# A hybrid decoder layer: two-operand work of the mixer off GpSimd, and early loads kept in program order

## The chip, the cores and the metric

The kernel runs on one core of a Trainium2 chip. The metric is device microseconds of one execution. A core has TensorE (PE: matmul, with its weight loads as PEld), VectorE (DVE), ScalarE (ACT), GpSimd (POOL) and SyncE (SP, which here only issues DMAs). Each engine works through its own instructions in order and waits on semaphores for the others.

## The reference

One layer of a hybrid decoder on 256 prompt tokens and 8 x 4 sample tokens (288 columns, T), width 2048, all in f32:

```python
def layer(x, pos, ssm0, conv0, kbuf, vbuf, mk, mv, lp):
    mix, ... = mixer(rmsnorm(x, lp['norm_mix']), pos, ssm0, conv0, kbuf, vbuf, lp)
    x = x + mix
    x = x + cross_attn(rmsnorm(x, lp['norm_x']), mk, mv, lp)
    x = x + ffn(rmsnorm(x, lp['norm_ffn']), lp)
```

The mixer projects its input to z, a convolution input (x, B, C), dt, q, k and v. Sixteen sliding-window attention heads (2 key heads, window 128, with sinks) and sixteen Mamba-2 heads (two groups, head size 64, state size 128, chunks of 128) run beside each other:

```python
    cs = jnp.cumsum(dtr * a, axis=2)
    wts = cb[..., None] * decay * dtr[:, :, None]
    y_diag = jnp.einsum('bctsgr,bcsgrp->bctgrp', wts, xr)
    to_end = jnp.exp(cs[:, :, -1:] - cs) * dtr
    chunk_states = jnp.einsum('bclgn,bclgrp->bcgrpn', br, xr * to_end[..., None])
    y_off = jnp.einsum('bclgn,bcgrpn->bclgrp', cr, h_starts) * jnp.exp(cs)[..., None]
```

The result is gated by silu(z), normed by group, joined with the attention output and projected by w_out. The outputs include the new states, the last convolution inputs and the key and value windows of prompt and samples. Memory cross-attention and a SwiGLU block of width 5632 follow.

## The kernel before, in words

**Matmul.** Activations stand transposed, one tile of 128 x 288 per 128 channels. Each weight is loaded as f32 (`wload`, line 147, into one of 3 `raw` buffers by SP), split into a rounded part `hi` by ACT (line 156) and a rest `lo` by DVE (through `tt`, line 79), with 4 buffers each, and three matmuls (lines 166 to 168) make one product. A chunk of 1024 weight columns is 24 such matmuls of 128 x 288. PSUM has 4 buffers for the projections (`mm`) and 4 for everything else (`ps`).

**Order.** The program is written out by hand as a chain of projections. Small work is put off by `later(n, fn)`: it runs `n` ticks on, and a tick is one weight chunk (`gemm_w` ends in `step(part=True)`, which takes at most half of what is due). A planner then orders each engine's instructions by priority and by when their inputs are ready: loads of weights stand 4000 places ahead, splits 70 ahead, so a load that needs nothing may be issued long before the place where it is written. SP and POOL are such queues as well: a DMA waits there behind the one ahead of it.

**Start.** `split_x` (line 277) transposes the input, splits it, and copies it (`xst`, 16 `xb` tiles) to be spilled to DRAM (`xspill`) by POOL; the same copies feed the dt product (line 421). The spill is read back into `xT` (line 1022) when the mixer's buffers are free, for the residual.

**Attention heads.** `swa_prompt` (line 494) rotates a pair of heads: shuffle, two products, a sum, the second product on POOL; `scores` follows a tick later, `values` three ticks behind that, `combine` one. `combine` writes `att`, which takes over the slots of `xst`. `swa_sample` (line 566) handles the samples against the cached keys, which it loads itself.

**Mamba heads.** `conv_state` (line 662) loads and transposes the convolution state; `conv_pair` convolves two channel tiles, with POOL copying the borders; `decay` and `decay2` make the masked decay matrices of four heads (POOL multiplies in `cbm`); `ssd` transposes x times dt (`nat_transpose`, line 712), makes the diagonal part (`diag`), has POOL scale it to the chunk's end (`decayed`), and goes on to `states` and `inter`. `sample_state` (line 848) goes over 16 pieces of state (two groups, two halves, four tiles): `load`, `grow` (POOL multiplies the old state by its decay), `trans` (four transposes and the update matmul of 512 columns, line 891, which DVE adds to the grown state), `read` and `add`. Its block-masked B (`bblk`) is masked on POOL and split by two ACT casts and one DVE operation. `part_done` counts the parts of a group; after five come `gate` and `group_norm`.

Of the kernel before, what the change touches and what calls it, by code (L numbers as in the profile page):

```python
# [46 lines left out]
def tile_hymba_step(ctx: ExitStack, tc: tile.TileContext, I: dict, O: list, stop: int = 99):  # L47
# [67 lines left out]
    def transpose(out, in_):  # L115
        k = in_.shape[0]
        b = in_.base_partition() if callable(in_.base_partition) else in_.base_partition
        nc.tensor.transpose(out, in_, ident[b:b + k, 0:k])  # L118

# [157 lines left out]
    def split_x(cp, pcs):  # L277
# [140 lines left out]
    pdt = psum()  # L418
    for k in range(KC):
        j = k % 4  # L420
        nc.tensor.matmul(pdt[32 * j:32 * j + 32, :T], wdt[:, k], xst[k], start=(k < 4), stop=(k >= KC - 4))
    dtT = ts()
    nc.scalar.copy(dtT, pdt[:, :T])
# [33 lines left out]
    def dt_sums():  # L457
# [17 lines left out]
        act(nat[:, 0, 3], pe[:, 48:64], AF.Exp)  # L475
        later(1, lambda: cs_natural(cs))
# [8 lines left out]

    later(1, dt_natural)
    later(7, dt_sums)


# [4 lines left out]
    def swa_prompt(r, pq):  # L494
# [60 lines left out]
        later(1, scores)  # L555
# [9 lines left out]

    def swa_sample():
        ms = cst[:, C_MS:C_MS + 144]
        kcT, vc = [], []
        for hb in range(2):
            k_ = tl(p_ld, [P, 4, P], F32, "ld")  # L570
            nc.sync.dma_start(k_, ck[4 * hb:4 * hb + 4].rearrange("b t g d -> t b (g d)"))
# [78 lines left out]

    later(7, swa_sample)
# [22 lines left out]
    def conv_pair(c0, pcs):  # L674
        ccs = []
        for j in range(2):
# [4 lines left out]
            nc.gpsimd.tensor_copy(smp(xr)[:, :, 0:3], scT[:, c].rearrange("p (b k) -> p b k", k=3))  # L681
# [11 lines left out]
            nc.gpsimd.tensor_copy(cc[:, 0:3], xr[:, 256:259])  # L693
            nc.gpsimd.tensor_copy(cc[:, 3:27].rearrange("p (b k) -> p b k", k=3), smp(xr)[:, :, 4:7])
# [17 lines left out]
    def nat_transpose(c0, h0=None):  # L712
        pts = [psum(), psum()]
        dst = [ts(256), ts(256), ts(256, TS)]
# [5 lines left out]
        for c, ps in enumerate((pts[0][:, 0:256], pts[0][:, 256:512], pts[1][:TS, 0:256])):  # L720
            if h0 is None:
                (nc.scalar.copy if c % 2 else nc.vector.tensor_copy)(dst[c], ps)
            else:
                n = CH[c][1] - CH[c][0]
                tt(nc.vector, hv_(dst[c]), hv_(ps), nat[:n, c, 0, h0:h0 + 4].unsqueeze(2).to_broadcast([n, 4, 64]),
                   ALU.mult)
        return dst

    bnat, cbm = [], []
    cmask = tm().rearrange("p (g b t) -> p g b t", g=2, b=NB)  # L730

    def bc_products():
        bnat.extend(nat_transpose(8))
        for c in range(3):
# [10 lines left out]
        for g in range(2):  # L745
            v = cmask[:, g].rearrange("p b (c t) -> p (b c) t", t=4)[:, 0:64:9]
            nc.gpsimd.tensor_copy(v, xc[10 + g][:, TP:T].rearrange("p (b t) -> p b t", t=4))
# [26 lines left out]
    def decay2(jj):  # L774
        sgv = sgs[jj]
        for c in range(3):
            n = CH[c][1] - CH[c][0]
            tt(nc.gpsimd, sgv[c], sgv[c], cbm[c][:, jj // 2].unsqueeze(1).to_broadcast([n, 4, n]), ALU.mult)

    def ssd(jj):  # L780
        g = jj // 2
        sgv = sgs[jj]
        xnat = nat_transpose(2 * jj, 4 * jj)

        def decayed(src, c, col, n=P):
            o_ = ts(256, n)
            tt(nc.gpsimd, hv_(o_), hv_(src),
               nat[:n, c, col, 4 * jj:4 * jj + 4].unsqueeze(2).to_broadcast([n, 4, 64]), ALU.mult)
            return o_

        def diag():
# [10 lines left out]
            xe = decayed(xnat[0], 0, 2)  # L802
            xe0, xe1 = decayed(xnat[0], 0, 3), decayed(xnat[1], 1, 2)
            xes = decayed(xnat[2], 2, 2, TS)
# [5 lines left out]
            later(2, lambda: states(xe, xe0, xe1))  # L810

        def states(xe, xe0, xe1):
# [634 lines left out]
```

## Time and profile before

| what | us |
|---|---|
| median of 3 timed runs (1396.06 to 1397.71) | 1396.43 |
| the profiled execution | 1390.5 |
| its span, first to last instruction | 1388.7 |
| PE busy in the span | 1367.5 |
| DVE busy | 806.5 |
| ACT busy | 638.0 |
| POOL busy | 177.6 |

The busy time of an engine is the time in which it works on an instruction; matmuls overlap, so PE's is no measure of its peak. In rows of grouped instructions, `out<-in` names the tiles, `xN` the count, then the busy time in us, the mean of one in ns, and the idle time just before with what ended it. Line 79 is the helper `tt`, line 82 `stt`, line 85 `act`, line 118 `transpose`, line 171 `split`.

### The profile page before, as it was taken

Reading aid. Unit: us, or ns where it says so; the run is one execution under the profiler, and the core shown is the slowest. Engines: PE = TensorE matmul, PEld = TensorE weight load, DVE = VectorE, ACT = ScalarE, POOL = GpSimd, SP = SyncE. Lnnn points to the kernel's source line nnn. Section 1 sums busy time; section 2 is a strip of 40 time slices with the busy share of each in tenths; the row PEclk is TensorE's granted clock in tenths of the full one; section 3 lists DMA queues with packets and bytes.
Section 4 is the critical chain, followed back from the end, with each engine's and each line's share of the span. In section 5 each row is a group of like instructions: output and inputs, shape, how many; then the busy total and the mean of one; then the engine's idle time right before and its main releaser. Section 6 shows DMA issues by size and latency. Waiting matters only on the chain.

```text
span 1388.7 us, 26190 instructions
## 1 busy us (share of the span) xinstructions
PE 1367.5 (98%) x10637; PEld 1331.8 (96%) x10637; DVE 806.5 (58%) x1341; ACT 638.0 (46%) x1001; POOL 177.6 (13%) x273
## 2 busy tenths in 40 slices
PE   9999999999999999999999999999999999999997
PEld 8899888988999899999999999999999999999997
DVE  6876798866566459554544544444454544545554
ACT  7455777655455446443343433333343343434332
POOL 4311465413120104000000000000000000000110
PEclk9999999999999999999999999999999999999999
DMA  9655558478557655555555555555555555555552
GB/s 296 169 158 154 143 151 242 134 223 214 165 177 245 221 163 162 167 167 167 168 168 167 168 160 166 167 167 175 167 167 168 167 167 167 168 160 167 167 167 92
DMA packets 249856, 241.17 MB, mean 174 GB/s; under 512 B 12778, under 2 KB 240528, under 8 KB 249736
## 3 DMA queue, kind: packets, MB, share of 16 engines
q1 hardware_dynamic: 246120, 232.43, 54.7%
q0 software_dynamic: 3584, 7.06, 1.7%
q8 instruction: 83, 1.36, 0.4%
q14 instruction: 37, 0.30, 0.1%
q10 hardware_dynamic: 32, 0.01, 0.0%
HBM read 227.59 MB, written 11.85 MB: 172 GB/s over the span
## 4 chain that ended last, share of the span: by engine, by line
PE 78%; DVE 3%; ACT 2%; issue 1%; POOL 1%; DMA 0%; DVEq 0%; ACTq 0%; POOLq 0%
PE mm L167 25%; PE mm L168 25%; PE mm L166 25%; PE ps L118 2%; POOL s L79 1%; DVE lo L79 1%; DVE xa L82 1%; ACT hi L156 0%; PE ps L1151 0%; DMA xT<-xspill 0%; DVE s L82 0%; ACT s L85 0%; POOL m L79 0%; DVE s L79 0%; ACT L85 0%
## 5 line engine op out<-in xcount | busy, mean ns | idle before, releaser
L79 DVE TENSOR_TENSOR lo<-raw,hi 128x1024 fp32r<-128x1024 f32 (+1 forms) x413 | 485.8, 1179 | 462.8 <-ACT hi L156 458.1
L156 ACT CAST hi<-raw 128x1024 fp32r<-128x1024 f32 (+1 forms) x413 | 410.5, 997 | 543.4 <-PE mm L168 442.4
L167 PE MATMUL mm<-xa,hi 128*128 128x288 f32 x2016 | 595.8, 296 | 0.0
L166 PE MATMUL mm<-xa,lo 128*128 128x288 f32 x2016 | 595.0, 295 | 0.6 <-ACT xa L171 0.6
L168 PE MATMUL mm<-xa,hi 128*128 128x288 f32 x2016 | 594.4, 295 | 0.0
L166 PEld LDWEIGHTS mm<-xa,lo 128*128 128x128 f32 x2016 | 380.1, 189 | 5.5 <-issue 3.8
L167 PEld LDWEIGHTS mm<-xa,hi 128*128 128x128 f32 x2016 | 378.8, 188 | 1.1 <-issue 0.7
L168 PEld LDWEIGHTS mm<-xa,hi 128*128 128x128 f32 x2016 | 378.7, 188 | 0.5 <-issue 0.3
L79 POOL TENSOR_TENSOR ssum<-ssum,ls 128x288 f32<-128x288 f32 x43 | 47.3, 1100 | 878.3 <-ACT ls L85 877.5
L166 PE MATMUL mm<-ls,lo 128*128 128x288 f32 x512 | 151.7, 296 | 0.0
L168 PE MATMUL mm<-ls,hi 128*128 128x288 f32 x512 | 151.4, 296 | 0.0
L167 PE MATMUL mm<-ls,hi 128*128 128x288 f32 x512 | 151.3, 295 | 0.0
L166 PE MATMUL mm<-xb,lo 128*128 128x288 f32 x448 | 132.8, 297 | 2.6 <-DVE xT L79 2.6
L167 PE MATMUL mm<-xb,hi 128*128 128x288 f32 x448 | 133.4, 298 | 0.0
L168 PE MATMUL mm<-xb,hi 128*128 128x288 f32 x448 | 132.7, 296 | 0.0
L166 PEld LDWEIGHTS mm<-ls,lo 128*128 128x128 f32 x512 | 96.2, 188 | 0.1
L167 PEld LDWEIGHTS mm<-ls,hi 128*128 128x128 f32 x512 | 96.2, 188 | 0.1
L168 PEld LDWEIGHTS mm<-ls,hi 128*128 128x128 f32 x512 | 96.2, 188 | 0.0
L166 PEld LDWEIGHTS mm<-xb,lo 128*128 128x128 f32 x448 | 85.1, 190 | 3.0 <-DVE xT L79 2.8
L168 PEld LDWEIGHTS mm<-xb,hi 128*128 128x128 f32 x448 | 85.3, 190 | 0.2 <-DVE xb L79 0.2
L167 PEld LDWEIGHTS mm<-xb,hi 128*128 128x128 f32 x448 | 84.7, 189 | 0.1
L79 DVE TENSOR_TENSOR xT<-xT,mm 128x288 f32<-128x288 f32 x64 | 28.3, 448 | 42.1 <-PE mm L168 37.5
(304 smaller groups left out, 1200.6 us busy)
## 6 DMA issues: line engine op xcount, KB each, us to landing
raw<-in_w_gate_dram SPq DMA_DIRECT2D x88, 512.0 KB, 3.6
raw<-in_w_up_dram SPq DMA_DIRECT2D x88, 512.0 KB, 3.6
raw<-in_w_down_dram SPq DMA_DIRECT2D x80, 512.0 KB, 3.6
raw<-in_w_in_dram SPq DMA_DIRECT2D x43, 512.0 KB, 3.9
raw<-in_w_in_dram SPq DMA_DIRECT2D x34, 256.0 KB, 4.6
raw<-in_w_out_dram SPq DMA_DIRECT2D x32, 256.0 KB, 4.2
raw<-in_w_out_dram SPq DMA_DIRECT2D x16, 512.0 KB, 3.5
ld<-in_state_ssm_dram SPq DMA_DIRECT2D x16, 256.0 KB, 4.8
```

Source lines behind the costliest of these rows:

```text
L79: eng.tensor_tensor(out=out, in0=in0, in1=in1, op=op)
L82: nc.vector.scalar_tensor_tensor(out=out, in0=in0, scalar=s, in1=in1, op0=op0, op1=op1)
L118: nc.tensor.transpose(out, in_, ident[b:b + k, 0:k])
L156: nc.scalar.copy(h_, src)
L166: nc.tensor.matmul(ps, wl, xh, start=start, stop=False)
L167: nc.tensor.matmul(ps, wh, xh, start=False, stop=False)
L168: nc.tensor.matmul(ps, wh, xl, start=False, stop=stop)
```

## The change

Three things are done. Products and sums of two tensors in the mixer go from POOL to DVE, or are folded into another operation; small copies go from POOL to ACT. The scaled inputs of `ssd` are made directly from the transposes in PSUM (with dt folded into the factors beforehand). The new state of the samples is made by four scalar-tensor-tensor operations of DVE instead of POOL's product and DVE's sum; B is split once for both groups (`b3`) and masked afterwards. And loads are tied to the program's order: `in_turn` puts a DMA behind the instruction written before it on its queue. With that the spill goes from POOL's queue to SP's, and it, the dt product, the cached keys and the first scores get other ticks.

```diff
+    def in_turn(ins):
+        tc.keep_in_program_order(ins)
...
             nc.vector.tensor_copy(st, pss[k][:, :T])
-            nc.gpsimd.dma_start(xspill[cp * 4 + k], st)
             xst.append(st)
...
-    nc.sync.dma_start(wdt[:, :, 0:16], wq[:, :, O_DT:O_DT + 16])
+    in_turn(nc.sync.dma_start(wdt[:, :, 0:16], wq[:, :, O_DT:O_DT + 16]))
...
+    def dt_product():
+        pdt = psum()
+        for k in range(KC):
+            j = k % 4
+            nc.tensor.matmul(pdt[32 * j:32 * j + 32, :T], wdt[:, k], xst[k], start=(k < 4), stop=(k >= KC - 4))
+        nc.scalar.copy(dtT, pdt[:, :T])
+        for k in range(KC):
+            later(1 + k // 2, lambda k=k: in_turn(nc.sync.dma_start(xspill[k], xst[k])))
+        later(1, dt_natural)
+        later(7, dt_sums)
...
+        tt(nc.vector, nat[:, :, 2], nat[:, :, 2], nat[:, :, 0], ALU.mult)
+        tt(nc.vector, nat[:, 0, 3], nat[:, 0, 3], nat[:, 0, 0], ALU.mult)
...
-    later(1, dt_natural)
-    later(7, dt_sums)
+    later(2, dt_product)
...
-        tt(nc.gpsimd, qb, qb, sq, ALU.mult)
+        tt(nc.vector, qb, qb, sq, ALU.mult)
         tt(nc.vector, qa, qa, qb, ALU.add)
-        nc.gpsimd.tensor_copy(qs[:, :, r], qa[:, TP:T].rearrange("p (b t) -> p b t", t=4))
+        nc.scalar.copy(qs[:, :, r], qa[:, TP:T].rearrange("p (b t) -> p b t", t=4))
...
-        later(1, scores)
+        later(2, scores)
...
+    def cache_keys():
+        for hb in range(2):
+            k_ = tl(p_ld, [P, 4, P], F32, "ld")
+            in_turn(nc.sync.dma_start(k_, ck[4 * hb:4 * hb + 4].rearrange("b t g d -> t b (g d)")))
+            kcs.append(k_)
...
+    later(3, cache_keys)
     later(7, swa_sample)
...
-            nc.sync.dma_start(scv[:24], I["state_conv"][0, :, :, 512 * cp:512 * cp + 512].rearrange("b k c -> (b k) c"))
+            in_turn(nc.sync.dma_start(scv[:24], I["state_conv"][0, :, :, 512 * cp:512 * cp + 512].rearrange(
+                "b k c -> (b k) c")))
...
-            nc.gpsimd.tensor_copy(cc[:, 0:3], xr[:, 256:259])
-            nc.gpsimd.tensor_copy(cc[:, 3:27].rearrange("p (b k) -> p b k", k=3), smp(xr)[:, :, 4:7])
+            nc.scalar.copy(cc[:, 0:3], xr[:, 256:259])
+            nc.scalar.copy(cc[:, 3:27].rearrange("p (b k) -> p b k", k=3), smp(xr)[:, :, 4:7])
...
+        for c, col in ((0, 0), (1, 0), (2, 0)) if h0 is None else NATS:
...
+                tt(nc.vector, hv_(d), hv_(ps), nat[:n, c, col, h0:h0 + 4].unsqueeze(2).to_broadcast([n, 4, 64]),
                    ALU.mult)
...
+    NATS = ((0, 0), (1, 0), (2, 0), (0, 2), (0, 3), (1, 2), (2, 2))
...
+        nc.scalar.copy(b3[0:32], bnat[2])
+        nc.scalar.copy(b3[32:64], bnat[2])
+        tt(nc.vector, b3[64:96], bnat[2], f32(b3[0:32]), ALU.subtract)
...
-            tt(nc.gpsimd, sgv[c], sgv[c], cbm[c][:, jj // 2].unsqueeze(1).to_broadcast([n, 4, n]), ALU.mult)
+            tt(nc.vector, sgv[c], sgv[c], cbm[c][:, jj // 2].unsqueeze(1).to_broadcast([n, 4, n]), ALU.mult)
...
-        xnat = nat_transpose(2 * jj, 4 * jj)
+        *xnat, xe, xe0, xe1, xes = nat_transpose(2 * jj, 4 * jj)
...
-                tt(nc.gpsimd, xc[i][:, P:TP], xc[i][:, P:TP], yo[:, j * P:(j + 1) * P], ALU.add)
+                tt(nc.vector, xc[i][:, P:TP], xc[i][:, P:TP], yo[:, j * P:(j + 1) * P], ALU.add)
...
-                nc.sync.dma_start(h0, ssm[4 * g + i4, :, 4 * hb:4 * hb + 4])
+                ld = nc.sync.dma_start(h0, ssm[4 * g + i4, :, 4 * hb:4 * hb + 4])
+                if g == 0 and hb == 0:
+                    in_turn(ld)
...
+            tt(nc.vector, bblk.rearrange("p (b n) -> p b n", b=4),
+               f32(b3[:, g * P:(g + 1) * P]).unsqueeze(1).to_broadcast([96, 4, P]),
+               bm[:, 4 * hb:4 * hb + 4].unsqueeze(2).to_broadcast([96, 4, P]), ALU.mult)
+            later(2, lambda: trans(hb, h0s, bblk))
...
-                hn = hns[i4]
-                tt(nc.vector, hn, hn, ps, ALU.add)
+                hn = tm()
+                for b in range(4):
+                    e_ = P + 16 * hb + 4 * b + 3
+                    stt(hn[:, b * P:(b + 1) * P], h0[:, b], ecs[i][:, e_:e_ + 1], ps[:, b * P:(b + 1) * P], ALU.mult,
+                        ALU.add)
...
-                tt(nc.gpsimd, xc[i][:, TP:T], xc[i][:, TP:T], yo[:, i4 * TS:i4 * TS + TS], ALU.add)
+                tt(nc.vector, xc[i][:, TP:T], xc[i][:, TP:T], yo[:, i4 * TS:i4 * TS + TS], ALU.add)
```

`swa_sample` then takes its keys from `kcs`; the copies of C into `cmask` and of the convolution state into `xr` go to ACT as well, and `bm` becomes a tile of 96 rows.

More of the change, by code (lines that the diff above doesn't have):

```diff
@@ L719, in nat_transpose @@
                 transpose(o_, xc[c0 + j][:, a:b_])
-        for c, ps in enumerate((pts[0][:, 0:256], pts[0][:, 256:512], pts[1][:TS, 0:256])):
+        dst = []
+        for c, col in ((0, 0), (1, 0), (2, 0)) if h0 is None else NATS:
+            ps = (pts[0][:, 0:256], pts[0][:, 256:512], pts[1][:TS, 0:256])[c]
+            n = CH[c][1] - CH[c][0]
+            d = ts(256, n)
+            dst.append(d)
             if h0 is None:
-                (nc.scalar.copy if c % 2 else nc.vector.tensor_copy)(dst[c], ps)
+                (nc.scalar.copy if c % 2 else nc.vector.tensor_copy)(d, ps)
             else:
-                n = CH[c][1] - CH[c][0]
-                tt(nc.vector, hv_(dst[c]), hv_(ps), nat[:n, c, 0, h0:h0 + 4].unsqueeze(2).to_broadcast([n, 4, 64]),
+                tt(nc.vector, hv_(d), hv_(ps), nat[:n, c, col, h0:h0 + 4].unsqueeze(2).to_broadcast([n, 4, 64]),
                    ALU.mult)
         return dst
+    NATS = ((0, 0), (1, 0), (2, 0), (0, 2), (0, 3), (1, 2), (2, 2))
+    bm = const.tile([96, 8], F32, name="bm")
+    for j in range(3):
+        nc.scalar.copy(bm[32 * j:32 * j + 32], cst[:TS, C_BM:C_BM + 8])
+    b3 = ts(256, 96, F32R)
     bnat, cbm = [], []
@@ L746, in bc_products @@
             v = cmask[:, g].rearrange("p b (c t) -> p (b c) t", t=4)[:, 0:64:9]
[L747 removed]
+            nc.scalar.copy(v, xc[10 + g][:, TP:T].rearrange("p (b t) -> p b t", t=4))
     ecs, xs3 = [None] * 8, [None] * 4
@@ L809, in diag, with states @@
             xs3[jj] = x3_
-            later(2, lambda: states(xe, xe0, xe1))
-        def states(xe, xe0, xe1):
+            later(2, states)
+        def states():
             ps = psum()
@@ L854, in load, with trans @@
                 h0 = tl(p_ld, [P, 4, P], F32, "ld")
[L855 removed]
+                ld = nc.sync.dma_start(h0, ssm[4 * g + i4, :, 4 * hb:4 * hb + 4])
+                if g == 0 and hb == 0:
+                    in_turn(ld)
                 h0s.append(h0)
[L857 to L860 removed]
             bblk = tm(n=96, dt=F32R)
[L862 to L877 removed]
+            tt(nc.vector, bblk.rearrange("p (b n) -> p b n", b=4),
+               f32(b3[:, g * P:(g + 1) * P]).unsqueeze(1).to_broadcast([96, 4, P]),
+               bm[:, 4 * hb:4 * hb + 4].unsqueeze(2).to_broadcast([96, 4, P]), ALU.mult)
+            later(2, lambda: trans(hb, h0s, bblk))
+        def trans(hb, h0s, bblk):
             if hb == 0:
```

39 lines of the change are left out of this document (3 added, 36 removed).

## The prediction, made before the result was known

> **What bounds the kernel now.** The profile's page comes first: the span and the share of each engine.
>
> ```profile
> span 1388.7 us, 26190 instructions
> ...
> PE 1367.5 (98%) x10637; PEld 1331.8 (96%) x10637; DVE 806.5 (58%) x1341; ACT 638.0 (46%) x1001; POOL 177.6 (13%) x273
> ```
>
> TensorE is busy for 98% of the span and no matmul is added or taken away, so the change can win only idle TensorE time: 1388.7 - 1367.5 = 21.2 us at most, plus what idling does to the clock. Next, the busy time by stretch: attention heads (40 to 142), Mamba heads with the output projection's start (142 to 332), and a plain stretch behind them.
>
> ```profile
> 40.00:142.00 102.00, 99.81 (x804) 91.67 (x803) 77.59 (x258) 51.54 (x141) 17.88 (x36) 0.98 0.57 157
> 142.00:332.00 190.00, 179.92 (x1492) 166.19 (x1491) 148.55 (x287) 126.20 (x216) 85.77 (x132) 1.00 0.63 179
> ...
> 360.00:380.00 20.00, 20.00 (x154) 20.00 (x153) 11.23 (x12) 8.39 (x12) 4.59 (x4) 1.00 0.62 172
> ```
>
> The columns are the window, its length, then busy us of PE, weight loads, DVE, ACT, POOL. TensorE idles 2.2 us in the first stretch and 10.1 us in the second. A matmul in the plain stretch takes 20/154 = 0.13 us, so a weight chunk (24 matmuls, one tick) 3.1 us. Third, the waits of TensorE name what it idles for (total, times, longest):
>
> ```profile
> PE mm L166 <- DVE xT L79: 2.6, 1, 2.6
> PE ps L511 <- DVE s L79: 2.2, 1, 2.2
> PE ps L891 <- ACT m L888: 1.7, 1, 1.7
> PE ps L118 <- DVE m L79: 1.4, 2, 0.9
> PE ps L833 <- ACT s L816: 1.3, 2, 0.8
> PE ps L216 <- DVE ld L214: 1.1, 1, 1.1
> PE ps L799 <- DVE s L79: 1.0, 1, 1.0
> PE mm L166 <- ACT xa L171: 0.6, 1, 0.6
> PE ps L943 <- DVE s L79: 0.6, 2, 0.4
> ```
>
> No row with a wait on a split weight (`lo`, `hi`) stands among them. Last, the stretches behind the two longest waits; the ninth number is the granted clock.
>
> ```profile
> 58.80:62.20 3.40, 3.40 (x15) 2.47 (x15) 3.26 (x19) 2.52 (x14) 3.14 (x6) 0.52 0.15 46
> ...
> 331.80:335.20 3.40, 3.40 (x16) 3.40 (x15) 3.40 (x8) 2.15 (x4) 3.38 (x7) 0.51 1.00 282
> ```
>
> Behind each wait over 2 us stand 3.4 us at half clock, which cost 3.4 x 0.48 = 1.6 us more; the 1.7 us wait has none behind it (the clock of 142 to 332 is 1.00, up to the dip at its end). So the wait of the first scores (L511) is worth 2.2 + 1.6 = 3.8 us. The Trainium skill, "TensorE: Matmul & The Clock Gate", section "What's actually happening", has the clock halve after an idle window of about 3.4 us. Here 2.2 us of idleness was enough, so the trace decides.
>
> **The change part by part. The first scores.** Now `scores` follows its projection after two ticks instead of one, its product with `sq` runs on DVE instead of POOL, and the dt product with its 17 small DVE operations begins two ticks later. The wait was for the sum `qa` on DVE. One tick puts 24 matmuls, 3.1 us, in front of the scores, more than the 2.2 us waited; DVE takes 0.451 us for the product (its 128x288 row below), and the hop to POOL and back goes. What comes late next is the dt chain, whose sums are planned seven ticks behind. I take -3.8 us, bounds 0 and -3.8.
>
> **Spill and loads.** The 16 spill writes leave POOL's queue in the first 40 us and go to SP, a tick or more after the dt product, two a tick; cache keys, conv state, dt weights and the first state tiles may no longer be issued ahead of the SP work written before them.
>
> ```profile
> ld<-in_state_ssm_dram SPq DMA_DIRECT2D x16, 256.0 KB, 4.8
> xspill<-xb POOLq DMA_DIRECT2D x16, 144.0 KB, 5.0
> ...
> 1.65 0.89 SPq L274 DMA_DIRECT2D ld<-in_x_prompt_dram  x2
> ...
> SPq L147 <- DVE lo L79: 672.5, 249, 13.1
> ```
>
> SP needs 0.89/2 = 0.45 us per issue, so 16 spills are 7 us of its time in 8 ticks (25 us), and it sits waiting for `raw` buffers (the last row: 672.5 us over the run). A pinned load that waits for an `ld` buffer holds the weight loads behind it; ACT's casts and DVE's splits then wait for those. The cover is three `raw` buffers, 3 x 3.1 = 9.3 us, against 4.8 us to landing. The attention output takes over a spilled tile's slot: head 0 is combined at tick 6, its spill is due at tick 3, 9.4 us against 5.0. I cost all of it at 0; without that cover it costs up to one landing, 4.8 us. The early transfers hold up no matmul now, so their going gains nothing directly.
>
> **POOL's products go to DVE.** Rows of DVE with their forms (count, busy us, mean ns), the second `lo` row from the plain stretch 600 to 750:
>
> ```profile
> L79 DVE TENSOR_TENSOR lo<-raw,hi 128x1024 fp32r<-128x1024 f32 x51 | 69.7, 1371 | 19.9 <-ACT hi L156 19.8
> L79 DVE TENSOR_TENSOR lo<-raw,hi 128x1024 fp32r<-128x1024 f32 x48 | 58.8, 1226 | 71.5 <-ACT hi L156 71.5
> L79 DVE TENSOR_TENSOR lo<-raw,hi 128x512 fp32r<-128x512 f32 x22 | 15.2, 705 | 4.2 <-ACT hi L156 4.2
> L79 DVE TENSOR_TENSOR m<-m,ps 128x512 f32<-128x512 f32 x16 | 10.7, 681 | 4.1 <-PE ps L891 3.9 <-POOL cc L693 0.2
> L79 DVE TENSOR_TENSOR m<-m,m 32x512 fp32r<-32x512 f32 x4 | 4.6, 1146 | 0.1
> L79 DVE TENSOR_TENSOR s<-mm,rstdb 128x288 f32<-128x288 f32 x10 | 4.3, 451 | 0.1
> L82 DVE SCALAR_TENSOR_TENSOR s<-s,hvec,ps 128x288 f32<-128x288 f32 x8 | 3.9, 506 | 0.5 <-PE ps L799 0.5
> L79 DVE TENSOR_TENSOR s<-ps,s 128x256 f32<-128x256 f32 x8 | 3.0, 418 | 2.4 <-PE ps L118 2.4
> L79 DVE TENSOR_TENSOR s<-ps,s 128x128 f32<-128x128 f32 x8 | 2.0, 280 | 6.6 <-PE ps L833 6.6
> L79 DVE TENSOR_TENSOR s<-ps,s 128x32 f32<-128x32 f32 x8 | 1.0, 184 | 1.6 <-PE ps L118 1.6
> ```
>
> Added to DVE between 142 and 332: the masked decay, 8 x 0.705 + 4 of 32x128 at about 0.27 (between the 128x32 and 128x256 rows) = 6.7; the four decayed inputs of each group, straight from PSUM, 16 x 0.418 = 6.7; the inter-chunk and sample sums, 8 x 0.280 + 8 x 0.184 = 3.7; the new state, where one sum of 512 columns becomes four scalar-tensor-tensor operations of 128. That form is not in the trace; 0.506 - (0.451 - 0.280) = 0.335, between 0.280 and 0.506, so 64 x 0.335 - 16 x 0.681 = +10.5. The block-masked B matrix, 4 x (0.705 - 1.146) + 0.4 = -1.4. Together +26.2 us. Back comes what POOL's neighbourhood costs DVE: `lo` takes 1.371 us here and 1.226 where POOL is quiet, 51 x 0.145 = 7.4 us, and more on other forms. DVE goes from 148.6 to about 167 of 190 us, 88%: fuller, not full. In the first stretch 8 x 0.451 = 3.6 us join 77.6 of 102. On ACT some 46 small copies (0.2 us, near its 128x32 row of 217 ns) come and eight casts go:
>
> ```profile
> L85 ACT ACT_TABLE_LOAD x23 | 29.5, 1283 | 0.4
> ...
> L85 ACT ACTIVATE s<-s 128x32 f32<-128x32 f32 x12 | 2.6, 217 | 0.0
> L862 ACT CAST m<-m 32x512 fp32r<-32x512 f32 x4 | 2.5, 612 | 2.0 <-POOL m L79 2.0
> ```
>
> 46 x 0.2 - 8 x 0.61 = +4 us on 126 of 190: hidden.
>
> What TensorE gains is latency. Its waits in the state stages (L891, L118, L833, L799, L943) sum to 1.7 + 1.4 + 1.3 + 1.0 + 0.6 = 6.0 us, and in each the last engine is DVE or ACT, often behind an operation that POOL stretched or fed. Bounds 0 and -6.0; I take half, **-3.0**, since the ACT side (23 table loads, ordered among the copies) stays. Against it stands the sample states' stage: each of the 16 pieces now holds its PSUM buffer for 4 x 0.335 = 1.34 us instead of 0.68. Today's loss there is L891 and L118, 3.1 us; if it grew with the piece it would double. With the stretching gone I take half of that, **+1.6** (bounds 0 and +10.5, all of the added DVE time on TensorE's path).
>
> **The end of the Mamba stage** (0.6 us on L171, 2.6 on `xT`, 1.6 of half clock) hangs on a chain of DVE and ACT operations of the second group norm, then on the loads of the spilled input:
>
> ```profile
> 330.31 0.46 DVE L79 TENSOR_TENSOR xT<-xT,mm 128x288 f32<-128x288 f32 x1 [4.48 <-DMA xT<-xspill]
> ```
>
> The change leaves the chain's tick as it is: 0.
>
> **Sum.** -3.8 - 3.0 + 1.6 = -5.2 us. The profiled execution took 1390.5 us (span 1388.7 and 1.8 around it); it would become 1385.3. The timed runs have a median of 1396.43, 5.9 above the profiled one, so I subtract there: **1391.2 us**.
>
> **Rivals.** *The state stage becomes DVE's (slower).* The price is the added 10.5 us on TensorE's path and two more stretches at half clock, 3.2, against -6.8: +6.9, 1403.3. It decides where fewer than five weight matmuls (0.66/0.13) stand between two pieces in TensorE's order. For it: 0.68 us more for each piece and 88% of DVE; against: a whole DVE stage free of POOL. *The waits only move*: the first scores or the dt chain wait a tick later, the state stages lose as before; 1396. For it: DVE has 81% in the first stretch. *A pinned load lands late* (the change does not bring its order about cheaply): one landing, 4.8, and a half-clock stretch, 1.6, on top of the forecast: 1397.6; against it the 9.3 us of cover. *More goes*: all 6.0 us of waits, and the end's chain comes early enough to lose its 0.6 and its half clock (1.6), without the 1.6 added: 1396.4 - 3.8 - 6.0 - 2.2 = 1384.4. *The clock does not follow the wait*: if the half clock behind the L511 wait has another cause, only 2.2 of the 3.8 go: 1392.8. Two waits over 2 us with two dips right behind them speak against it. The Trainium skill, "TensorE: Matmul & The Clock Gate", section "What's actually happening", would read it so, a wait of 2.2 us being shorter than its window.
>
> **Chances.** Forecast 0.44 (own range 1388.5 to 1394), more goes 0.16, clock does not follow 0.04, waits move 0.14, late load 0.07, slower 0.15. A measurement can tell about 0.2%, 2.8 us, from no change. Faster by that (under 1393.6): 0.42 of the forecast's 0.44 + 0.16 + 0.04 = 0.62; slower (over 1399.2): 0.15 + 0.01 of the late loads = 0.16; the rest, 0.02 + 0.14 + 0.06 = 0.22, is the same. The range reaches to 1384 below and, leaving out the dear half of the slower case, to 1400 above.
>
> **What would show it.** Right: no wait on L511 and no half clock near 60; `lo` near 1226 ns everywhere; L799 and L833 waits under half; the `xT` wait still there. Wrong: L891 or L118 waiting on DVE for over 3 us together, a new wait on a DMA at the conv-state transposes, or TensorE waiting for `lo`. A transfer or a full DVE ahead of the weights would make the prediction wrong altogether.

## The result, and the profile after

The changed kernel took 1381.67 us (median of 4 runs, 1380.41 to 1382.05) against 1396.55 us (4 runs, 1396.06 to 1397.71): a ratio of 0.9897, 95% interval 0.9882 to 0.9911. It gained 14.9 us where 5.2 were forecast, and lies under the range (1384 to 1400). Its profiled execution took 1382.05 us.

The page of the changed kernel, first lines:

```profile
span 1380.3 us, 26140 instructions
...
PE 1367.6 (99%) x10637; PEld 1334.1 (97%) x10637; DVE 810.5 (59%) x1444; ACT 638.4 (46%) x1042; POOL 84.4 (6%) x139
```

TensorE is busy as long as before (1367.5). Its idle time fell from 21.2 to 1380.3 - 1367.6 = 12.7 us. All its waits that are left (total, times, longest):

```profile
PE mm L169 <- DVE xT L79: 2.8, 1, 2.8
PE ps L219 <- DVE ld L217: 1.1, 1, 1.1
PE mm L169 <- ACT xa L174: 0.6, 1, 0.6
PE mm L118 <- DVE ld L1384: 0.2, 1, 0.2
PE ps L954 <- DVE s L79: 0.2, 1, 0.2
```

The first scores' wait and every wait over 0.2 us of the state stages are gone; those of the stage's end, 0.6 and 2.8 us, stayed. (Lines have moved by 3 and more: the weight matmuls of L166 to L168 are now L169 to L171.) By stretch, with the columns as before (PE, weight loads, DVE, ACT, POOL, then the granted clock), and the stretches at and behind the `xT` wait:

```profile
316.00:319.00 3.00, 0.18 (x3) 0.03 (x1) 0.54 (x2) 0.00 (x1) 1.53 (x4) 1.00 1.02 271
319.10:322.50 3.40, 3.33 (x24) 3.10 (x25) 3.40 (x7) 3.00 (x6) 3.40 (x8) 1.00 0.92 245
40.00:142.00 102.00, 102.00 (x842) 95.12 (x842) 82.98 (x274) 58.24 (x162) 11.62 (x25) 1.00 0.63 176
142.00:332.00 190.00, 186.28 (x1550) 173.51 (x1549) 155.47 (x387) 125.72 (x240) 13.03 (x31) 1.00 0.68 196
```

POOL went from 85.77 to 13.03 us in the Mamba stretch; DVE took its products over and rose only from 148.55 to 155.47, where 167 were forecast. TensorE's idle time there is 3.72 us, nearly all of it the `xT` wait and the 0.6 us ahead of it. And behind 2.8 us of waiting the granted clock stayed at 1.00. The groups of DVE that the forecast spoke of:

```profile
L79 DVE TENSOR_TENSOR lo<-raw,hi 128x1024 fp32r<-128x1024 f32 x55 | 66.8, 1217 | 14.3 <-ACT hi L159 14.0
L82 DVE SCALAR_TENSOR_TENSOR m<-ld,s,ps 128x128 f32<-128x128 f32 x64 | 17.5, 342 | 4.6 <-PE ps L899 4.2
```

`lo` has come down from 1371 to 1217 ns, and the new scalar-tensor-tensor form takes 342 ns, where 335 were estimated.

Between the two profiled executions the change gained 1390.5 - 1382.05 = 8.45 us, as much as the idle time fell (8.5). The other 6.4 us lie between the executions that were timed and the one that was profiled, so that was tried first.

### The profile page after: what moved, and what is told of

The parts are those of the page before. It is cut to its first block, busy times and chain, and to the rows that moved or that the text cites. A ratio compares the mean times of both kernels' runs of the same rounds, so it can differ in the third digit from the quotient of the medians.

```text
span 1380.3 us, 26140 instructions
## 1 busy us (share of the span) xinstructions
PE 1367.6 (99%) x10637; PEld 1334.1 (97%) x10637; DVE 810.5 (59%) x1444; ACT 638.4 (46%) x1042; POOL 84.4 (6%) x139
## 4 chain that ended last, share of the span: by engine, by line
PE 96%; DVE 2%; ACT 1%; issue 1%; DMA 0%; POOL 0%; DVEq 0%; ACTq 0%; POOLq 0%
PE mm L169 29%; PE mm L170 29%; PE mm L171 29%; PE ps L118 3%; DVE xa L82 1%; PE ps L823 0%; DVE lo L79 0%; PE ps L521 0%; DMA xT<-xspill 0%; PE ps L1162 0%; ACT hi L159 0%; PE ps L899 0%; PE ps L1197 0%; PE ps L912 0%; PE ps L1235 0%
## 5 line engine op out<-in xcount | busy, mean ns | idle before, releaser
L79 DVE TENSOR_TENSOR lo<-raw,hi 128x1024 fp32r<-128x1024 f32 (+1 forms) x413 | 478.1, 1160 | 449.4 <-ACT hi L159 444.4
L169 PE MATMUL mm<-xa,lo 128*128 128x288 f32 x2016 | 599.8, 298 | 0.6 <-ACT xa L174 0.6
L171 PE MATMUL mm<-xa,hi 128*128 128x288 f32 x2016 | 590.3, 293 | 0.0
L169 PEld LDWEIGHTS mm<-xa,lo 128*128 128x128 f32 x2016 | 378.0, 187 | 4.8 <-issue 3.1
L171 PEld LDWEIGHTS mm<-xa,hi 128*128 128x128 f32 x2016 | 379.1, 188 | 1.0 <-issue 0.7
L169 PE MATMUL mm<-ls,lo 128*128 128x288 f32 x512 | 152.4, 298 | 0.0
L171 PE MATMUL mm<-ls,hi 128*128 128x288 f32 x512 | 151.6, 296 | 0.0
L169 PE MATMUL mm<-xb,lo 128*128 128x288 f32 x448 | 132.2, 295 | 2.9 <-DVE xT L79 2.8
L171 PE MATMUL mm<-xb,hi 128*128 128x288 f32 x448 | 131.9, 294 | 0.0
L169 PEld LDWEIGHTS mm<-ls,lo 128*128 128x128 f32 x512 | 96.6, 189 | 0.1
L171 PEld LDWEIGHTS mm<-ls,hi 128*128 128x128 f32 x512 | 96.3, 188 | 0.0
L169 PEld LDWEIGHTS mm<-xb,lo 128*128 128x128 f32 x448 | 84.6, 189 | 3.6 <-DVE xT L79 3.4
L171 PEld LDWEIGHTS mm<-xb,hi 128*128 128x128 f32 x448 | 84.6, 189 | 0.2 <-DVE xb L79 0.2
```

Of the source, the lines that this page charges most:

```text
L79: eng.tensor_tensor(out=out, in0=in0, in1=in1, op=op)
L169: nc.tensor.matmul(ps, wl, xh, start=start, stop=False)
L171: nc.tensor.matmul(ps, wh, xl, start=False, stop=stop)
```

## The experiments

Each was timed beside the kernel before on the same chip, and each ratio is to that kernel. Its medians there were 1392.79 us (experiments 1 to 4), 1396.54 (5 to 8), 1394.5 (9 to 11) and 1395.57 (12 and 13).

**1. The kernel before, once more.** No edit.

> The kernel before, unchanged. Its timed runs took 1396.5 us, its profiled execution 1390.5; the changed kernel's agree within 2 us. Theory one: the timed executions have more stretches at half clock than the profiled one (a wait of TensorE near 2 us does or does not meet the clock's window); then executions near 1396 show a granted clock under 0.995, by about 12 us of half clock (0.991). Theory two: the waits themselves are longer in them (POOL and DVE meet differently); then the clock stays at 0.995 and the span grows by idle time. Either way the median should be 1396 again.

It took 1391.39 to 1399.21 us (10 runs, median 1396.35). Runs of 1397 us and more had a mean granted clock of 0.992 or 0.993, runs under 1394 one of 0.996 or 0.997. The same kernel beside it, on the same chip, had a median of 1392.79 us (31 runs): two groups of one kernel can lie 3.6 us apart, as they have more or fewer executions at the low clock, so smaller differences between medians below say little by themselves. Its profiled execution took 1398.13 us, 7.6 more than the one shown ahead of the prediction. The waits were the same (`xT` 2.9, first scores 2.8, then 1.7, 1.4, 1.0, 1.0); what differed were stretches at half clock (a granted clock near 0.50). By windows, with the stretch ahead of the second one:

```profile
61.00:64.40 3.40, 3.40 (x15) 2.75 (x15) 3.40 (x23) 3.27 (x16) 2.32 (x4) 0.50 0.18 51
166.80:170.20 3.40, 3.40 (x35) 2.57 (x33) 3.40 (x12) 2.90 (x5) 2.97 (x3) 1.00 0.01 3
170.20:177.00 6.80, 6.80 (x33) 6.04 (x32) 6.80 (x9) 4.84 (x7) 5.33 (x5) 0.50 0.40 105
214.60:218.00 3.40, 3.40 (x15) 3.21 (x14) 3.40 (x2) 2.16 (x4) 3.40 (x5) 0.50 1.01 298
337.40:340.80 3.40, 3.40 (x17) 3.40 (x16) 3.40 (x7) 1.99 (x4) 3.38 (x7) 0.51 0.94 248
...
600.00:800.00 200.00, 200.00 (x1514) 200.00 (x1514) 100.05 (x124) 77.25 (x94) 0.00 (x0) 1.00 0.55 166
```

The four rows at 0.50 and 0.51 add up to 17.0 us at half clock, against 6.8 in the earlier profile: 10.2 x 0.5 = 5.1 us more. The two in the middle, at 170 and 214, stand in the Mamba stretch, where the earlier execution had none. The one at 214 follows the wait of 1.7 us, which had no half clock behind it in the earlier profile; the one at 170 follows no wait, for TensorE counts as busy through all of the 3.4 us ahead of it (30 of its 35 matmuls there are small ones of the sample attention). Most of the rest is in the last row, a stretch of plain weight matmuls, beside the same window of the earlier profile:

```profile
600.00:800.00 200.00, 200.00 (x1528) 200.00 (x1527) 102.56 (x128) 78.82 (x96) 0.00 (x0) 1.00 0.55 169
1000.00:1200.00 200.00, 200.00 (x1527) 200.00 (x1526) 101.49 (x127) 78.92 (x96) 0.00 (x0) 1.00 0.54 167
```

At a clock of 1.00 a matmul takes 200/1528 = 0.1309 or 200/1514 = 0.1321 us there, one of two paces; 14 matmuls fewer are 14 x 0.131 = 1.8 us. So 5.1 + 1.8 = 6.9 of the 7.6 us are found. The kernel before has no single time: it spreads over some 8 us with the stretches at half clock that an execution meets. On all four chips its runs of 1396 us and more had a clock of 0.992 to 0.994, so the first comparison (1396.06 to 1397.71), whose clocks are not known, is taken to have had many too.

**2. The state stages alone**, with the start put back (rotation on POOL, scores after one tick, spill from POOL, dt product at once).

```diff
+            nc.gpsimd.dma_start(xspill[cp * 4 + k], st)
...
-    later(2, dt_product)
+    dt_product()
...
-        tt(nc.vector, qb, qb, sq, ALU.mult)
+        tt(nc.gpsimd, qb, qb, sq, ALU.mult)
...
-        later(2, scores)
+        later(1, scores)
```

> The changed kernel with the attention start put back: spill on POOL in the start, dt product at once, first scores after one tick, rotary product and q copy on POOL. My theory, by waits: the wait of the first scores (2.2 us) and its half clock (1.6) come back and nothing else, 1381.7 + 3.8 = 1385.5. Rival: the start holds most of what the timed runs gained, 1390 or more. Rival: the start is worth nothing by itself, 1382.

1389.65 us (1383.74 to 1394.38), ratio to the kernel before 0.9971 [0.9951, 0.9992]. Waits of TensorE:

```profile
PE mm L169 <- DVE xT L79: 2.8, 1, 2.8
PE ps L611 <- DVE stx L615: 1.4, 1, 1.4
PE ps L520 <- DVE xb L79: 1.2, 1, 1.2
```

No wait over 0.2 us of the Mamba heads' states is left. A wait of 1.4 us is new at the sample attention's scores (L611), with half clock right behind it (149 to 160 us) and again at 173 to 180. At the first scores, near 58 us, only 0.2 us came back, and no half clock (the 1.2 us of L520 stand at 112). So the forecast that their wait alone returns was wrong. The lowest time, 1383.74, came at a clock of 0.997, the highest at 0.991.

**3. The start alone**, in the kernel before.

```diff
-            nc.gpsimd.dma_start(xspill[cp * 4 + k], st)
...
+    later(2, dt_product)
...
-        tt(nc.gpsimd, qb, qb, sq, ALU.mult)
+        tt(nc.vector, qb, qb, sq, ALU.mult)
...
-        later(1, scores)
+        later(2, scores)
```

> The kernel before with only the attention start changed: spill on SP behind the dt product, dt product two ticks on, first scores after two ticks, rotary product on DVE, cached keys pinned. My theory: 3.8 us less than before, 1392.7, with the waits of the state stages as before. Rival (start holds most): 1386 or less. If both parts only work together: 1396.

1394.64 us (1389.78 to 1396.14), ratio 1.0004 [0.999, 1.0017]: nothing gained. Its waits, the largest first:

```profile
PE mm L169 <- DVE xT L79: 2.8, 1, 2.8
PE ps L849 <- ACT s L832: 1.9, 2, 1.1
PE ps L118 <- ACT s L85: 1.8, 2, 1.6
PE ps L907 <- ACT m L904: 1.5, 1, 1.5
...
PE ps L610 <- DVE stx L614: 0.9, 1, 0.9
```

The first scores' wait is gone and there is no half clock near 60. But there is a new wait of 0.9 us at the sample attention (L610), with half clock behind it at 147 to 151 us and again at 168 to 171, and the state stages wait as before. In this profile the loss has moved; why it moves there was not tried.

**4. The changed kernel without any pin** (`in_turn` does nothing).

```diff
-        tc.keep_in_program_order(ins)
+        return ins
```

> The changed kernel with the pins removed: the loads and the spills may again be issued whenever their inputs are there. My theory: the pins are worth nothing on TensorE's path, since weights were never late: 1382 within 2.8 us. Rival: floated loads crowd the first 60 us and delay weights there, and the first wait over 2 us comes back: 1385.5 or more.

1383.84 us (1380.59 to 1392.25), ratio 0.9943 [0.9921, 0.9964]. Three of ten runs took 1389.9 to 1392.25 us, at a clock of 0.991; the profile is of one of these. The other seven took 1380.59 to 1386.89. A wait of 1.1 us stands at L612, and this window behind it (6.8 us more at half clock follow at 171):

```profile
147.00:157.20 10.20, 10.04 (x53) 8.78 (x53) 5.54 (x23) 9.17 (x23) 0.17 (x2) 0.50 0.65 213
```

These are three stretches of 3.4 us in a row, and TensorE counts as busy for 10.04 of the 10.20 us: the second and third follow one in which it hardly idled. Its work there is small matmuls, those of the sample attention above all, among weight matmuls (23 of the 53).

**5. POOL's old products, once more and for nobody.** The changed kernel computes, besides, the masked decay, the scaled inputs and the grown states on POOL into tiles that are not read.

```diff
+            junk = tm()
+            jv = junk[:n, 0:4 * n].rearrange("p (h t) -> p h t", h=4)
+            tt(nc.gpsimd, jv, sgv[c], cbm[c][:, jj // 2].unsqueeze(1).to_broadcast([n, 4, n]), ALU.mult)
...
+            for i4 in range(4):
+                junk = tm()
+                tt(nc.gpsimd, junk.rearrange("p (b n) -> p b n", b=4), h0s[i4],
+                   ecs[4 * g + i4][:, e_:e_ + 13:4].unsqueeze(2).to_broadcast([P, 4, P]), ALU.mult)
```

> The changed kernel with POOL's old products of the Mamba stage (masked decay, scaled inputs, grown states) computed once more on POOL into tiles that nobody reads; everything else as in the changed kernel. Theory one (what POOL does beside DVE stretches DVE and so makes the waits): lo of 128x1024 goes from 1217 ns back to 1330 or more, waits of 0.5 us and over come back in the state stages, 2 to 4 us together, and the time rises by 2 to 5 us at equal clock. Theory two (the waits came from the operations that stood in a chain through POOL): lo is stretched as well, but nothing in the chain is, no wait over 0.4 us comes back in the state stages, and the time changes by less than 1 us.

1397.8 us (1390.79 to 1401.93, 12 runs), ratio 1.0016 [0.9996, 1.0036]: 15.6 us over the changed kernel's 1382.18 on the same chip, three times the most that was expected. The whole gain is lost by work that nothing waits for. Its largest waits:

```profile
PE ps L118 <- DVE s L82: 4.4, 1, 4.4
PE mm L169 <- DVE xT L79: 2.6, 1, 2.6
PE ps L911 <- DVE s L79: 1.3, 1, 1.3
```

`lo` is hardly stretched (1253 ns, not the 1330 expected). Single operations are. The timeline of DVE (start, length in us) shows an addition of two SBUF tiles of 128x128, one that takes 0.28 us elsewhere:

```profile
198.78 6.34 DVE L79 TENSOR_TENSOR s<-s,s 128x128 f32<-128x128 f32 x1
```

and the timeline of POOL the six products that run meanwhile:

```profile
198.89 6.07 POOL L79 TENSOR_TENSOR m<-ld,s 128x512 f32<-128x512 f32 x6
```

The addition ends at 205.12, just after the sixth product (204.96): DVE stood still for it, and the transposes (L118), which need what is queued behind it on DVE, waited 4.4 us. Half clock follows at 206 to 210. The kernel before shows the same smaller, first POOL, then DVE:

```profile
210.48 3.05 POOL L79 TENSOR_TENSOR m<-ld,s 128x512 f32<-128x512 f32 x3
```

```profile
211.34 3.28 DVE L79 TENSOR_TENSOR lo<-raw,hi 128x1024 fp32r<-128x1024 f32 x1
```

A split of 1.22 us takes 3.28 and ends at 214.62, 1.1 us after POOL's last product (213.53): it began in earnest only about then. No wait of TensorE follows this one within 15 us. The added products also take buffers, which was not told apart, so the 15.6 us are no measure of what POOL cost before (it is busy for 53.59 us of the Mamba stretch here, 85.77 in the kernel before). That its work beside DVE can make a wait, with half clock behind it, is shown by the held addition.

The largest wait of the state stages in the kernel before (L891, 1.7 us, for ACT's copy) came another way, in a chain through POOL. First ACT, then TensorE:

```profile
203.44 0.41 ACT L806 CAST s<-s 32x256 fp32r<-32x256 f32 x1 [3.42 <-POOL s L79]
...
209.45 0.50 PE L891 MATMUL ps<-m,s 96*128 96x512 f32 x1 [1.67 <-ACT m L888]
```

ACT stood 3.42 us for POOL's products (the scaled inputs) and was then busy, two table loads of 1.28 us included, until its copy came. In the changed kernel those inputs come from DVE.

**6. The first rows early** (a version of its own): the first two tiles of the spilled input have buffers of their own and are read back by SP before the Mamba stage ends; the mixer's pool has 15 buffers instead of 16.

```diff
+    xT0 = [tl(xe_pool, [P, T], F32, f"xT{k}") for k in range(2)]
...
-    mixm = tc.tile_pool(name="mixm", bufs=16, side="right")
+    mixm = tc.tile_pool(name="mixm", bufs=15, side="right")
...
+    for k in range(2):
+        tc.keep_in_program_order(nc.sync.dma_start(xT0[k], xspill[k]))
```

> The changed kernel with the first two tiles of the spilled input read back into buffers of their own by SP before the Mamba stage ends. Theory one (TensorE's wait of 2.8 us for xT is for the transfer that can start only when the mixer's buffers are free): the wait goes or falls under 0.5 us, and the time falls by 2 to 3 us at equal clock. Theory two (behind the transfer stands another chain, the second group norm): the wait moves to another operation within the next microsecond, and the time falls by less than 1 us.

1373.95 us (1373.56 to 1376.47), ratio 0.9858 [0.9836, 0.988], 8.2 us under the changed kernel on the same chip: the best version. Its windows, where the `xT` wait was and in the later stretches:

```profile
316.00:322.00 6.00, 6.00 (x48) 6.00 (x47) 3.71 (x6) 3.00 (x6) 3.81 (x8) 1.00 0.93 254
...
1000.00:1200.00 200.00, 200.00 (x1527) 200.00 (x1527) 102.61 (x128) 78.19 (x96) 0.00 (x0) 1.00 0.55 168
```

The wait is gone and did not move. That is 2.0 us; the half clock behind it, which experiment 7 has, is another 1.7; the shorter pace in the last window (1527 matmuls, 1514 in experiment 7) gives 13 x 0.131 = 1.7. These are 5.4 of the 5.9 us between the two spans (1380.2 and 1374.3); why the pace differs stays open. So the wait is worth 2.0 us and what lies behind it, not the whole 8.2.

**7. The changed kernel, once more.**

> The changed kernel unchanged, for the spread of its times beside its granted clock. Theory one (two losses: waits, which the change takes away for good, and stretches at half clock, which come and go with the execution): the times spread from about 1380 at a mean clock of 0.998 to about 1390 at 0.991, the median lies between, 1382 to 1386, and at equal clock the kernel is 8 to 9 us under the one before (the 8.5 us of idle time between the two profiles). Theory two (the change has also taken the half clock away): all runs stay at 1380 to 1383 with a clock of 0.997 or more.

1382.18 us (1378.94 to 1382.96), ratio 0.9907 [0.9886, 0.9928], clock 0.997 or 0.998 in all six. So, by their clock, the half clock is nearly away in all ten runs of the changed kernel. The profile has one stretch of it:

```profile
318.40:321.80 3.40, 3.40 (x16) 3.40 (x15) 3.40 (x8) 2.39 (x5) 3.31 (x8) 0.50 0.95 270
...
1000.00:1200.00 200.00, 200.00 (x1514) 200.00 (x1514) 99.75 (x123) 76.83 (x92) 0.00 (x0) 1.00 0.54 166
```

Here the `xT` wait of 2.0 us has half clock behind it, where the first profile's wait of 2.8 us had none.

**8. The grown states on POOL again**, in a tick of their own, with one DVE sum of 512 columns.

```diff
-            later(2, lambda: trans(hb, h0s, bblk))
+            later(1, lambda: grow(hb, h0s, bblk))
...
-                    stt(hn[:, b * P:(b + 1) * P], h0[:, b], ecs[i][:, e_:e_ + 1], ps[:, b * P:(b + 1) * P], ALU.mult,
-                        ALU.add)
+                hn = hns[i4]
+                tt(nc.vector, hn, hn, ps, ALU.add)
```

> The changed kernel with one part undone: the new state of the samples is grown on POOL in a tick of its own and DVE adds one row of 512 columns (0.68 us a piece) instead of four scalar-tensor-tensor operations (4 x 0.342 = 1.37 us). Theory one (the piece's longer hold of its PSUM buffer costs nothing, since DVE has 20% of the stage to spare; POOL's work is what costs): waits in the sample states' stage come back on the sum or the transposes, 0.5 to 2 us together, and the time rises by 0 to 2 us. Theory two (the prediction's term: the longer hold costs 1.6 us): the time falls by about 1.6 us, with no waits at the pieces.

1384.24 us (1380.33 to 1385.84), ratio 0.992 [0.9897, 0.9943]: 2.1 us more than experiment 7, not 1.6 less; the two groups of six overlap, so only the absence of a gain is clear. The one new wait of size is 2.0 us, not at the pieces; the timeline of ACT has a weight load just before it:

```profile
190.06 1.04 ACT L159 CAST hi<-raw 128x1024 fp32r<-128x1024 f32 x1 [4.28 <-DMA raw<-in_w_in_dram]
191.01 0.53 ACT L85 ACTIVATE s<-s 128x256 f32<-128x256 f32 x2
```

ACT's split waited 4.28 us for weights that SP issued late (185.22 us on its timeline, 182.87 in the changed kernel), and what TensorE's transposes need stood behind the split. SP had waited 4.3 us for a buffer that DVE's `lo` held, and DVE was late because five products of POOL (174.38 to 182.83 us) stretched its convolution:

```profile
179.44 1.23 DVE L82 SCALAR_TENSOR_TENSOR s<-s,cwT,s 128x312 f32<-128x312 f32 x1
```

The same operation takes 0.53 us once POOL is done. In the changed kernel the four scalar-tensor-tensor operations of a piece show no wait at all.

**9. The scores after one tick.**

```diff
-        later(2, scores)
+        later(1, scores)
```

> The changed kernel with one part undone: the first scores follow their projection after one tick again, their rotation still on DVE alone. Theory one (the tick is what covers the rotation): TensorE's wait for the rotated heads comes back near 60 us, 1 to 2 us, shorter than the old 2.2 since the hop to POOL is gone, and now and then with a stretch at half clock behind it; the time rises by 1 to 3.5 us. Theory two (POOL's product was the late one): with it on DVE one tick is enough, no wait, time within 1 us of the changed kernel.

1388.22 us (1382.85 to 1392.29, clock 0.990 to 0.998), ratio 0.9951 [0.9928, 0.9973]. Both theories missed. TensorE does not idle between 40 and 70 us: with the rotation on DVE one tick is enough. Yet the time is 7.7 us over experiment 10, which had the changed kernel's time, and the loss stands much later, at 148 us, with half clock at 148 to 151, at 168 to 175 and behind the `xT` wait:

```profile
PE ps L612 <- DVE stx L616: 1.1, 1, 1.1
```

**10. The cached keys unpinned.**

```diff
-            in_turn(nc.sync.dma_start(k_, ck[4 * hb:4 * hb + 4].rearrange("b t g d -> t b (g d)")))
+            nc.sync.dma_start(k_, ck[4 * hb:4 * hb + 4].rearrange("b t g d -> t b (g d)"))
```

> The changed kernel with the two loads of cached keys free to be issued ahead of the SP work written before them; spill, conv state, dt weights and first state tiles stay in program order. Theory one (what the kernel without any pins lost, 1.1 us at the sample attention and 10 us at half clock behind it, hangs on the keys): the wait in 145 to 150 us comes back and some executions show a clock of 0.991 and 1390 us. Theory two (it hangs on the first state tiles): the time stays within 1 us of the changed kernel, clock 0.997 or more in all.

1380.49 us (1379.01 to 1382.38), ratio 0.9901 [0.9883, 0.992], clock 0.997 or 0.998: this pin is worth nothing.

**11. The first state tiles unpinned.**

```diff
-                if g == 0 and hb == 0:
-                    in_turn(ld)
```

> The changed kernel with the loads of the first state tiles free to be issued early; all other pins stay. Theory one (an early state tile sits in an ld buffer and the next one waits for such a buffer at the head of SP's queue, so that the cached values behind it land late): the loads of the cached values are issued some 4 us later than in the changed kernel, TensorE waits 1 us or more at the sample attention, and some executions show a clock of 0.991 and about 1390 us. Theory two (the pins make no difference, as the prediction had it): the time stays within 1 us of the changed kernel, clock 0.997 or more.

1386.35 us (1380.71 to 1388.87, clock 0.991 to 0.997), ratio 0.9934 [0.9912, 0.9957]: 5.9 us over experiment 10. TensorE waits 0.9 us at L612 (145.7 us), and in this profile 6.8 us at half clock stand 20 us later, at 165 to 172 us. SP issues the tiles in the attention stretch, and the cached values right behind one of them (129.98 us in the changed kernel):

```profile
100.55 2.56 SPq L875 DMA_DIRECT2D ld<-in_state_ssm_dram  x3
...
132.80 0.37 SPq L875 DMA_DIRECT2D ld<-in_state_ssm_dram  x1
133.21 1.05 SPq L596 DMA_DIRECT2D m<-in_cache_swa_v_dram  x2
```

The values go out again from POOL's queue, and behind that issue, 3.05 us of it, stands a small memset of the convolution. POOL's timeline, experiment 11:

```profile
137.06 3.05 POOL L598 DMA_DIRECT2D out_dram<-m  x2 [40.78 <-DMA m<-in_cache_swa_v_dram]
140.09 0.12 POOL L699 MEMSET s<- 128x3 f32 x1
```

and of the changed kernel:

```profile
136.27 3.05 POOL L598 DMA_DIRECT2D out_dram<-m  x2 [40.14 <-DMA m<-in_cache_swa_v_dram]
139.31 0.12 POOL L699 MEMSET s<- 128x3 f32 x1
```

0.8 us of delay (the values were issued 3.2 us later and landed 0.8 us later), passed on to ACT's convolution, to DVE and to the sample scores.

**12. The same, with the convolution's memsets on DVE.**

```diff
-            nc.gpsimd.memset(xr[:, 0:3], 0.0)
+            nc.vector.memset(xr[:, 0:3], 0.0)
...
-            nc.gpsimd.memset(ac[:, n:], 0.0)
+            nc.vector.memset(ac[:, n:], 0.0)
```

> The kernel with the first state tiles unpinned, with one thing more: the two small memsets of the convolution (L699 and L708, 128x3) run on DVE instead of POOL. Theory one (the chain there runs from the cached values, which land late, through POOL's two issues of their write-out, 3.05 us, behind which the memsets stand, to ACT's convolution, to DVE and to the sample scores): ACT's wait of 2.6 us for the memset goes, so does TensorE's wait of 0.9 us at L612, and the time falls by 2 to 6 us to that of the changed kernel, about 1381, with a clock of 0.996 or more in most executions. Theory two (POOL is not in that chain; the early state tiles hold ld buffers that others need): wait and time stay as with the first state tiles unpinned, 1386.

1383.92 us (1381.87 to 1384.18), ratio 0.9917 [0.9896, 0.9938], clock 0.997 or 0.998 in all. ACT's convolution follows at once:

```profile
137.20 0.63 ACT L85 ACTIVATE s<-s,vT,cwT 128x312 f32<-128x312 f32 x1
```

at 137.20 where POOL's memset alone had come at 140.09. The wait at L612 is gone, and so is all half clock between 40 and 345 us: the chain of that wait goes through POOL's write-out. That the half clock comes from that wait is argued, not shown: experiment 1 has the stretch at 170 us without it. Part of the gain goes into a new wait:

```profile
PE mm L169 <- DVE xT L79: 2.8, 1, 2.8
PE ps L118 <- ACT m L894: 1.4, 1, 1.4
```

**13. Experiment 6 with the memsets on DVE**, the edit of 12.

> The kernel with the first two tiles of the spilled input read back early (1374 us), with the same two memsets on DVE. Theory one: nothing waits for POOL's memsets in that kernel in a way that reaches TensorE, so the time stays within 1 us of it. Theory two: the convolution comes earlier on ACT and with it the sample attention; the stretch of small matmuls is spread otherwise, and a stretch at half clock appears or goes, 2 us or more.

1378.42 us (1377.93 to 1380.0), ratio 0.9883 [0.9862, 0.9903], 4.5 us over experiment 6 (on another chip; the kernel before took 1.0 us less there). Where the chain was no bound, moving it only made a wait of 2.0 us for ACT elsewhere (L118, at 213 us), with half clock behind it.

## Why the prediction was wrong

**The bound** was read rightly as far as idle time goes: 8.5 of the 21.2 us went. What half clock takes was counted only behind two waits.

**The first scores** (-3.8). In the changed kernel wait and half clock are gone, as forecast. But not as a term that adds: alone the start is worth nothing (experiment 3, the rival that the waits only move), and the second tick's worth lies at the sample attention (experiment 9, 7.7 us), not at the scores. Of the two reasons given, taking the product from POOL to DVE is enough there; whether the tick alone would have covered the hop was not tried.

**The state stages** (-3.0, +1.6). Here a term failed: "I take half". Of the 6.0 us 5.8 went, and the +1.6 did not come; undoing the four operations brought no gain (experiment 8). The half that was left standing was charged to ACT and its table loads. Of these 19 are still there between 142 and 332 us, of 22 before, and the waits are gone; the largest had ACT late behind POOL's products (experiment 5). The prediction read POOL's cost off the mean of `lo` (1371 against 1226) and priced it as DVE time, 7.4 us. That was too little: over the shortest of its form, the DVE operations of that stretch took 24.8 us more in the kernel before and 8.1 in the changed one, 16.7 us less, which goes far to explain why DVE came to 155.47 us and not to 167. (The 51 splits of the sum stand between 40 and 332 us; the 40 of them in the Mamba stretch, at 1411 ns, give the same 7.4 by chance.) And the mean hides the tail: one operation held for microseconds (6.3 in experiment 5) makes a wait of TensorE.

**Spill and pins** (0). True of the cached keys (experiment 10); of the spill no run speaks by itself. Not true of the first state tiles: 5.9 us, through a load behind a load, POOL's queue and a memset. The prediction looked for the harm of a pin at the weight loads; the harm of an early load, and what stood behind it, it did not follow.

**The end of the stage** (0) was right: the `xT` wait is still there.

**The sum** failed last and by most: "The timed runs have a median of 1396.43, 5.9 above the profiled one, so I subtract there". That took the 5.9 us for a constant. They are, for the most part, stretches at half clock: an execution like the timed ones shows 17.0 us of them where the profiled one has 6.8. The changed kernel's two profiles have none and one, and all ten of its runs a clock of 0.997 or 0.998, so these 6 us went too: 8.5 + 6.4 = 14.9. In the profiled pair the same does not show, since the two stretches at half clock that went (6.8 x 0.49 = 3.3 us) are made up for by the longer pace of matmuls in the execution after, 13 fewer in each of two windows, 26 x 0.131 = 3.4 us:

```profile
600.00:800.00 200.00, 200.00 (x1515) 200.00 (x1514) 101.46 (x127) 78.51 (x96) 0.00 (x0) 1.00 0.54 166
1000.00:1200.00 200.00, 200.00 (x1514) 200.00 (x1514) 99.80 (x123) 76.85 (x92) 0.00 (x0) 1.00 0.54 166
```

**The clock rule** ("Behind each wait over 2 us stand 3.4 us at half clock") is refuted: in the changed kernel none stands behind 2.8 us in one execution and one behind 2.0 us in another, the 1.7 us wait has one in experiment 1 and none in the first profile, and the one at 170 us there follows no wait. Two instances were taken for a rule. The Trainium skill's page "TensorE: Matmul & The Clock Gate", section "What's actually happening", also has the window free-running, so that where it falls varies; the prediction passed over that sentence, and experiments 1 and 7, in which one kernel meets half clock at a wait in one execution and not in another, agree with it.

Of the rivals, "more goes" (1384.4) was nearest, in number and in mechanism: the waits of the state stages went without the 1.6 added. "The clock does not follow the wait" was right in its doubt and not in its number (1392.8). The slower one, the state stage as DVE's, is refuted by the changed kernel's own waits, none of which stands at the pieces.

Open: why an earlier tick of the scores delays the cached values (133.70 us in experiment 9, with no state tile before them), what brings half clock to the sample attention in one execution and not in another, and what sets the pace of the plain matmuls.

## What to carry to other kernels

When timed runs lie above the profiled one, find out what that distance is before you subtract from it: compare the granted clocks of single runs, since behind a wait of one microsecond there can stand several more at half clock (experiment 4). Price an engine's work beside another by all forms that it stretches and by the longest held operation, not by the mean of one form. And a queue that carries both transfers and small operations of a chain (here POOL's memset behind a write-out) is part of that chain.

## What the runs showed of the hardware

**DVE can stand still through a run of POOL's products.** A DVE operation on two SBUF tiles stood for 6.3 us until six products of POOL were done (experiment 5). The Trainium skill, "SBUF — State Buffer", section "Who interferes with whom", says that a DVE instruction with two inputs in SBUF contends with a GpSimd instruction that reads SBUF, and calls the contention an exclusive lock. The trace agrees for this addition, and adds that the loser may stay blocked through several instructions in a row.

**Half clock without idleness.** Stretches of 3.4, 6.8 and 10.2 us at 0.50 came, and one of 6.8 us behind 3.4 us in which TensorE counts as busy throughout, with 30 small matmuls out of 35 (experiment 1). The same kernel meets them in one execution and not in another: 1389 to 1399 us for the kernel before.

**Two paces at full clock.** 0.1309 or 0.1321 us for the same plain matmuls, for hundreds of microseconds on end, differing between executions of one kernel (experiment 1 against the first profile).
